# Spreading the pooling projections of a decoder block among the last heads' key and gate projections

## The chip, the cores and the metric

The kernel runs on one core of one Trainium2 chip (trn2). The metric is the device time of one execution in microseconds. A core has a matrix engine (PE, with its weight loads shown apart as PEld), a vector engine (DVE), a scalar engine (ACT), GpSimd (POOL) and a queue engine (SP) that here only issues transfers. Every engine works through its own instructions in a fixed order and waits, by semaphores, for what it needs from the others.

## The reference: one decoder block, 512 rows of width 1024

```python
h = rms_norm(x, g_mix);  u, q, k, v, gate_logits = split(h @ w_in)
y_pool = pool(u, w_pool) * pool_scale   # moving means over 2, 4, 8, 16 rows, minus u, then 128x128 weights, 4 groups
o      = diff_attention(rope(q), rope(k), v)   # 4 heads; softmax 1 - lam * softmax 2, causal
y_attn = rms_norm(o, g_subln) * (1 - lam_init)
x = x + (concat([y_pool, y_attn]) * sigmoid(gate_logits)) @ w_out
x = x + cross_attention(rms_norm(x), rms_norm(mem));  x = x + relu(rms_norm(x) @ w_up)**2 @ w_down
return rms_norm(x, g_final)
```

Everything is fp32. A product is made of three fp32r matmuls: both operands are split into a rounded high part and a low rest (`split`, lines 110 to 112: ACT writes the high part, DVE or POOL subtracts it for the low part), and `mm3` (lines 104 to 107) adds high x high, high x low and low x high.

## The kernel before

The part in question is the first quarter of the program. After the projection of v, twenty weight tiles follow, each a projection of all 512 rows to 128 columns: 24 matmuls of 128x512 into one of two `acc` banks. Their order is the string `PLAN`, read at line 302 and run by the loop at line 561: `k0` to `k3` and `q0` to `q3` are the heads' keys and queries, `u0` to `u3` the four pooling groups, `g0` to `g7` the gates (0 to 3 belong to the pooling groups, 4 to 7 to the heads). I number the tiles 0 to 19 by their place in `PLAN`.

What a tile is followed by:

- a key or query (`qk_proj`, lines 412 to 432): four ACT copies and one DVE product drain the bank, POOL makes two operations of the rotary embedding (lines 419, 420), ACT and DVE write the split pair `s`. For a key two transfers on SP (lines 430, 431) write a swapped copy `z`. All these live in six buffers with the tag `s`.
- a gate (`gate_proj`, lines 494 to 507): DVE line 498, ACT lines 500 to 502, DVE line 503, ACT line 504. `merge` (lines 509 to 514) multiplies it into its group's or head's result and splits the product: on POOL for groups 0 to 3, on DVE for the heads.
- a pooling group (`u_proj`, lines 524 to 545): DVE line 532 drains the bank, POOL adds shifted copies (line 537: 1, 2, 3 and 4 adds for groups 0 to 3), DVE line 540 and two narrow operations (lines 542, 543) finish the means, ACT and POOL split them. `u0` first calls `pool_weights` (lines 517 to 522): a transfer and a split of the pooling weights into an `s` buffer. 23 steps later `pool_mix` (lines 547 to 557) runs three matmuls into a `tr` bank, and ACT line 554 drains it.

The attention is laid between the tiles by a step counter. `tile_mm` counts one step for every three matmuls, so a tile has 8 steps; `after` (line 271) queues a function for a later step. With `START, SPACE, SOFTMAX, ATTEND, FINISH, POOLING = 20, 6, 15, 3, 6, 23` (line 32) the scores of head h and row block i stand at step 36 + 6(4h + i), their transposes (`flip`, line 456) 15 steps later, `attend` (line 469) 3 steps after a head's last flip, and `finish` (line 481) 6 steps after that. Scores write into three `sc` banks in turn, which DVE line 445 drains; a flip's transposes go to one of two `tr` banks, which ACT and DVE split into `at` (lines 465, 111, 112), and `attend` multiplies `at` with v. I write (h,i) for head h and row block i.

The order on PE is the order in which the program is written. The orders on the other engines and queues are set when the program is built. Weights come through three raw buffers and three split buffers (`load`, `prep`, `weights`, lines 155 to 213): at tile i the load of tile i+3 and the split of tile i+2 are asked for. The projection of the mixed result (`projection`, lines 580 to 595, called at line 662) follows the twentieth tile; its first three tiles take the parts 4, 5, 6, 0, 1 first and 2, 7, 3 last.

## Time and profile before

| | before |
|---|---|
| device time, three runs | 724.32, 724.35, 726.61 us; median 724.35 |
| the profiled execution: its own time, its span | 725.17 us, 723.4 us |
| DVE, ACT, POOL busy in the span | 513.1, 391.6, 72.9 us |
| DMA | 91.09 MB, mean 126 GB/s |
| line 105, 106, 107 `acc` matmuls of 128x512 on `whi`, `wlo` | 400 each, 395, 389, 390 ns |
| line 111 on ACT (`whi`, 94 of them), line 112 on DVE (`wlo`, 94) | mean 1035 ns, 1229 ns |

The span runs from the first to the last instruction of the profiled execution; 1.77 us of its own time lie around it. Matmuls overlap: one of 128x512 is shown with some 0.39 us, but the next one starts 0.23 us later, so on PE I read the distance between starts, not the durations. In a row of a timeline the first number is the start, the second the duration, and the bracket at the end gives the idle time before the instruction and who ended it. On DVE and ACT, too, the next instruction may start a little before the last one's shown end.

### The profile page before, as it was taken

What the parts mean: (1) busy time and instruction counts of PE and PEld (TensorE: products, weight loads), DVE (VectorE), ACT (ScalarE), POOL (GpSimd) and SP (SyncE); (2) the same over time, 40 slices, a digit from 0 to 9 for tenths busy, and PEclk for the clock granted to TensorE, in tenths of its full rate; (3) what the DMA queues carried; (4) which work ended last, traced back from release to release, by engine and by line L of the source; (5) the groups of instructions that cost most, each with busy time, mean ns of one, the idle gap of its engine ahead of it and who ended that gap; (6) DMA issues with size and microseconds to landing.
All of it is one profiled execution on the core that took longest, in us unless ns stands there. A gap on an engine that the chain in (4) does not pass through costs nothing.

```text
span 723.4 us, 10277 instructions
## 1 busy us (share of the span) xinstructions
PE 705.2 (97%) x3960; PEld 612.8 (85%) x3960; DVE 513.1 (71%) x798; ACT 391.6 (54%) x642; POOL 72.9 (10%) x66
## 2 busy tenths in 40 slices
PE   9999999999999999999999999999999999999993
PEld 6887888788889888888879978999889988899882
DVE  6698999975888545562899954598447963589426
ACT  7498998676766433452775641355214641355422
POOL 0044112534000000000000000000000000000003
PEclk9999999999999999999999999999999999999997
DMA  8443223143525552114835741548226651305003
GB/s 314 151 117 116 88 74 116 59 151 112 175 88 178 179 166 88 59 58 144 238 86 141 236 147 30 167 108 279 88 42 163 216 166 55 101 17 178 27 1 116
DMA packets 28256, 91.09 MB, mean 126 GB/s; under 512 B 3088, under 2 KB 5136, under 8 KB 28208
## 3 DMA queue, kind: packets, MB, share of 16 engines
q1 hardware_dynamic: 25856, 81.92, 33.7%
q0 software_dynamic: 2352, 8.52, 7.0%
q8 instruction: 31, 0.51, 0.3%
q14 instruction: 17, 0.14, 0.1%
HBM read 86.24 MB, written 2.10 MB: 122 GB/s over the span
## 4 chain that ended last, share of the span: by engine, by line
PE 78%; DVE 11%; ACT 4%; DMA 3%; issue 2%; POOL 0%; SPq 0%; DVEq 0%; ACTq 0%
PE acc L105 16%; PE acc L107 16%; PE acc L106 16%; PE sc L105 9%; PE sc L107 8%; PE sc L106 8%; DMA mraw<-wst 2%; DVE wlo L112 2%; DVE mix L112 1%; PE sc L386 1%; ACT tmp L447 1%; DVE mix L849 1%; PE sc L388 1%; PE sc L390 1%; DMA wraw<-wm 1%
## 5 line engine op out<-in xcount | busy, mean ns | idle before, releaser
L105 PE MATMUL acc<-xg,whi 128*128 128x512 f32 x400 | 158.2, 395 | 0.0
L107 PE MATMUL acc<-xg,wlo 128*128 128x512 f32 x400 | 156.1, 390 | 0.0
L106 PE MATMUL acc<-xg,whi 128*128 128x512 f32 x400 | 155.8, 389 | 0.0
L111 ACT CAST whi<-wraw 128x1024 fp32r<-128x1024 f32 (+1 forms) x94 | 97.1, 1035 | 106.5 <-PE acc L106 39.0
L112 DVE TENSOR_TENSOR wlo<-wraw,whi 128x1024 fp32r<-128x1024 f32 (+1 forms) x94 | 115.3, 1229 | 26.8 <-ACT whi L111 26.4
L107 PEld LDWEIGHTS acc<-xg,wlo 128*128 128x128 f32 x400 | 75.1, 188 | 16.1
L105 PEld LDWEIGHTS acc<-xg,whi 128*128 128x128 f32 x400 | 75.2, 188 | 14.7
L106 PEld LDWEIGHTS acc<-xg,whi 128*128 128x128 f32 x400 | 75.2, 188 | 14.5
L572 DVE TENSOR_TENSOR vr<-acc,vr 128x512 f32<-128x512 f32 x41 | 28.3, 691 | 82.3 <-PE acc L107 82.3
L164 POOL DMA_DIRECT2D mraw<-wst x16 | 13.8, 861 | 429.6 <-DMA mraw<-wst 292.2
L105 PE MATMUL sc<-mix,whi 128*128 128x256 f32 (+1 forms) x184 | 54.2, 294 | 0.0
L107 PE MATMUL sc<-mix,wlo 128*128 128x256 f32 (+1 forms) x184 | 54.0, 293 | 0.0
L106 PE MATMUL sc<-mix,whi 128*128 128x256 f32 (+1 forms) x184 | 53.9, 293 | 0.0
L111 ACT CAST whi<-mraw 128x1024 fp32r<-128x1024 f32 x24 | 25.0, 1051 | 43.3 <-PE acc L106 30.7
L885 DVE TENSOR_TENSOR tmp<-sc,tmp 128x512 f32<-128x512 f32 x56 | 37.7, 689 | 6.4 <-PE sc L107 6.3
L106 PE MATMUL acc<-xg,mhl 128*128 128x512 f32 x104 | 40.6, 390 | 0.2 <-DVE xg L112 0.2
L105 PE MATMUL acc<-xg,mhl 128*128 128x512 f32 x104 | 40.6, 391 | 0.0
L107 PE MATMUL acc<-xg,mhl 128*128 128x512 f32 x104 | 40.5, 390 | 0.0
L111 ACT CAST mhl<-wraw 128x1024 fp32r<-128x1024 f32 x19 | 20.0, 1053 | 33.9 <-PE acc L106 18.0
L107 PEld LDWEIGHTS sc<-mix,wlo 128*128 128x128 f32 x184 | 34.6, 188 | 1.1
L105 PEld LDWEIGHTS sc<-mix,whi 128*128 128x128 f32 x184 | 34.5, 188 | 1.0
L106 PEld LDWEIGHTS sc<-mix,whi 128*128 128x128 f32 x184 | 34.4, 187 | 1.1
(269 smaller groups left out, 1696.4 us busy)
## 6 DMA issues: line engine op xcount, KB each, us to landing
wraw<-wm SPq DMA_DIRECT2D x76, 512.0 KB, 3.6
mraw<-wst SPq DMA_DIRECT2D x24, 512.0 KB, 3.6
wraw<-wckv SPq DMA_DIRECT2D x16, 512.0 KB, 3.8
mraw<-wst POOLq DMA_DIRECT2D x16, 512.0 KB, 5.8
wraw<-wst SPq DMA_DIRECT2D x16, 512.0 KB, 3.7
s<-s SPq DMA_DIRECT2D x8, 256.0 KB, 3.7
vr<-xT SPq DMA_DIRECT2D x8, 256.0 KB, 4.8
outT<-mix SPq DMA_DIRECT2D x8, 256.0 KB, 2.2
```

Of the source, the lines that this page charges most:

```text
L105: nc.tensor.matmul(o, lh, rh, start=start, stop=False)
L106: nc.tensor.matmul(o, lh, rl, start=False, stop=False)
L107: nc.tensor.matmul(o, ll, rh, start=False, stop=stop)
L111: S.copy(hi, src)
L112: eng.tensor_tensor(lo, src, f(hi), op=ALU.subtract)
L164: nc.gpsimd.dma_start(r, part(n, then), accum_op=ALU.add)
L386: nc.tensor.matmul(o[i], xg[k][0][:, tb], wh[:, c], start=k == 0, stop=False)
L388: nc.tensor.matmul(o[i], xg[k][1][:, tb], wh[:, c], start=False, stop=False)
L390: nc.tensor.matmul(o[i], xg[k][0][:, tb], wl[:, c], start=False, stop=k == KC - 1)
L447: S.activation(e[:, :n], e[:, :n], AF.Exp, bias=mn, scale=-1.0, accum_out=sm[:, c:c + 1])
L572: V.tensor_tensor(t, o, t, op=ALU.add)
L885: V.tensor_tensor(u[new], o, u[old], op=ALU.add)
```

## The change

One string is written in another order.

```diff
-PLAN = "k0 q0 q1 k1 q2 q3 g4 k2 g5 g6 k3 g7 u0 u1 u2 u3 g0 g1 g2 g3"
+PLAN = "k0 q0 q1 k1 q2 q3 g4 k2 g5 u0 k3 g6 u1 g7 u2 g0 u3 g1 g2 g3"
```

Tiles 0 to 8, tile 10 (`k3`), tile 14 (`u2`) and the last three keep their places. `u0` moves from tile 12 to 9, `u1` from 13 to 12, `u3` from 15 to 16; `g6` from 9 to 11, `g7` from 11 to 13, `g0` from 16 to 15. The step numbers of the attention stay as they are. Nothing is added or left out: each engine has as many instructions as before. The matmuls of `pool_mix` for group 0 move with `u0` from step 127 to step 103, that is from behind the scores (3,3) to ahead of the scores (3,0). On the other engines the instructions behind the moved tiles change places. Three such places:

The first is on DVE, around the drains of the score banks of (3,0), `sc_322` and `sc_325` before. `tr_329` is the flip of (2,2), `acc_316` the tile `u1`, `wlo_340` the low part of the weights of tile 15, `tmp_307` the result of head 1.

```order
L112 TENSOR_TENSOR at_296_1216<-tr_329_1337,at_295_1215 128x3x128
L532 TENSOR_TENSOR padu_330_1346<-acc_316_1285,rstd_61_315 128x512
L445 ISA tmp_323_1313,small_324_1314<-sc_322_1310,cst_2_68 128x128
L445 ISA small_324_1314 128x1
L511 TENSOR_TENSOR tmp_307_1252<-tmp_307_1252,gate_219_925 128x512
L112 TENSOR_TENSOR wlo_340_1367<-wraw_317_1286,whi_339_1366 128x1024
L445 ISA tmp_326_1320,small_327_1321<-sc_325_1317,cst_2_68 128x128
```

The same place now: the banks of (3,0) are `sc_329` and `sc_332`, `tr_336` is the flip of (2,2), `acc_323` the tile `g7`, `tmp_311` head 1's result, `wlo_342` the low part of the weights of tile 16.

```order
L112 TENSOR_TENSOR at_300_1222<-tr_336_1352,at_299_1221 128x3x128
L498 TENSOR_TENSOR gate_337_1361<-acc_323_1300,rstd_61_315 128x512
L225 SCALAR_TENSOR_TENSOR tmp_311_1258<-tmp_312_1259,tmp_311_1258 128x512
L531 MEMSET padu_403_1615 128x16
L112 TENSOR_TENSOR wlo_342_1373<-wraw_324_1301,whi_341_1372 128x1024
L445 ISA tmp_330_1328,small_331_1329<-sc_329_1325,cst_2_68 128x128
L445 ISA small_331_1329 128x1
L511 TENSOR_TENSOR tmp_311_1258<-tmp_311_1258,gate_219_925 128x512
L445 ISA tmp_333_1335,small_334_1336<-sc_332_1332,cst_2_68 128x128
```

The first drain of (3,0) stood ahead of the weights' low part and stands behind it now; the two drains stand closer together.

The second is on DVE, a little later, around the low part of the flip of (2,3), the last that `attend` of head 2 needs (`tr_349` before, `tr_351` now). `acc_337` before and `acc_339` now are the tile `u2`. Before:

```order
L112 TENSOR_TENSOR at_296_1216<-tr_349_1404,at_295_1215 128x4x128
L531 MEMSET padu_393_1556 128x16
L452 SCALAR_TENSOR_TENSOR tmp_323_1313<-tmp_323_1313,small_321_1309,tmp_326_1320 128x128
L445 ISA tmp_343_1380,small_344_1381<-sc_342_1377,cst_2_68 128x256
L445 ISA small_344_1381 128x1
L532 TENSOR_TENSOR padu_364_1458<-acc_337_1363,rstd_61_315 128x512
```

Now:

```order
L503 SCALAR_TENSOR_TENSOR gate_337_1361<-gate_337_1361,tmp_338_1363 128x512
L452 SCALAR_TENSOR_TENSOR tmp_330_1328<-tmp_330_1328,small_328_1324,tmp_333_1335 128x128
L532 TENSOR_TENSOR padu_366_1464<-acc_339_1369,rstd_61_315 128x512
L112 TENSOR_TENSOR at_300_1222<-tr_351_1410,at_299_1221 128x4x128
L445 ISA tmp_355_1430,small_356_1431<-sc_354_1427,cst_2_68 128x384
```

The flip's low part stood ahead of the drain of tile `u2` and stands behind it now.

The third is on POOL, from the first add of group 3 (`padu_393` before, `padu_403` now) to the merges of groups 0 and 1. Before:

```order
L537 TENSOR_TENSOR pad_394_1559<-padu_393_1556 128x512
L537 TENSOR_TENSOR pad_395_1562<-pad_394_1559 128x512
L537 TENSOR_TENSOR pad_396_1565<-pad_395_1562 128x512
L537 TENSOR_TENSOR pad_397_1568<-pad_396_1565 128x512
L112 TENSOR_TENSOR tmp_400_1576<-tmp_398_1571,tmp_399_1575 128x512
L511 TENSOR_TENSOR s_392_1551<-s_392_1551,gate_409_1626 128x512
L112 TENSOR_TENSOR mix_411_1635<-s_392_1551,mix_411_1635 128x512
```

Now:

```order
L537 TENSOR_TENSOR pad_404_1618<-padu_403_1615 128x512
L511 TENSOR_TENSOR s_315_1278<-s_315_1278,gate_394_1561 128x512
L537 TENSOR_TENSOR pad_405_1621<-pad_404_1618 128x512
L112 TENSOR_TENSOR mix_396_1570<-s_315_1278,mix_396_1570 128x512
L537 TENSOR_TENSOR pad_406_1624<-pad_405_1621 128x512
L537 TENSOR_TENSOR pad_407_1627<-pad_406_1624 128x512
L112 TENSOR_TENSOR tmp_410_1635<-tmp_408_1630,tmp_409_1634 128x512
```

Group 0's merge, two instructions, stood behind group 3's adds and stands between them now. On DVE, group 3's lines 540, 542 and 543 now stand directly ahead of the low part of head 3's squares, which `finish` of head 3 needs; before, five instructions stood between.

## The prediction

> **What bounds the kernel now.** I read the page's busy shares first, then PE's waits between 80 and 200 us, where the moved tiles lie, then PE's order of time around each wait.

> ```profile
> PE 705.2 (97%) x3960; PEld 612.8 (85%) x3960; DVE 513.1 (71%) x798; ACT 391.6 (54%) x642; POOL 72.9 (10%) x66
> PEclk9999999999999999999999999999999999999997
> ```

> PE is busy 97% of the span at a granted clock of 0.9 or more in all slices but the last. The change gives PE the same matmuls in another order, so all that it can win or lose is waiting.

> ```profile
> PE sc L442 <- DVE small L445: 1.0, 2, 0.7
> PE av L106 <- DVE at L112: 0.7, 2, 0.4
> ```

> Four waits for DVE: two of scores for a free bank, two of `attend` for a flip's low part. Idle time hides the cost of restarting the pipeline, so I read the starts:

> ```profile
> 107.56 0.40 PE L105 MATMUL av<-at,vr 128*128 128x512 f32 x1
> 108.28 0.50 PE L106 MATMUL av<-at,vr 128*128 128x512 f32 x1 [0.33 <-DVE at L112]
> ...
> 124.95 0.28 PE L442 MATMUL sc<-s,s 128*128 128x256 f32 x1
> 125.07 0.28 PE L443 MATMUL sc<-s,s 128*128 128x256 f32 x1
> 125.55 0.38 PE L442 MATMUL sc<-s,s 128*128 128x256 f32 x1 [0.20 <-DVE small L445]
> ...
> 130.49 0.33 PE L442 MATMUL sc<-s,s 128*128 128x384 f32 x1
> 130.66 0.34 PE L443 MATMUL sc<-s,s 128*128 128x384 f32 x1
> 131.75 0.44 PE L442 MATMUL sc<-s,s 128*128 128x384 f32 x1 [0.75 <-DVE small L445]
> ...
> 148.33 0.39 PE L107 MATMUL acc<-xg,wlo 128*128 128x512 f32 x1
> 148.56 0.40 PE L105 MATMUL acc<-xg,whi 128*128 128x512 f32 x1
> ```

> A matmul of 512 columns takes 0.23 us from start to start (148.33 to 148.56), of 256 columns 0.12, of 384 columns 0.17. Against these steps the waits cost 0.72 - 0.23 = **0.49** (attend of head 1), 0.48 - 0.12 = **0.36** (second scores of (3,1)) and 1.09 - 0.17 = **0.92** (second scores of (3,2)): 1.77 us together. The fourth wait, at 85 us in attend of head 0, lies ahead of the first moved tile and stays.

> ```profile
> 80.00:100.00 20.00, 19.59 (x97) 16.07 (x97) 17.43 (x43) 19.73 (x45) 2.59 (x2) 1.00 0.32 93
> 100.00:120.00 20.00, 19.67 (x96) 16.22 (x95) 18.77 (x42) 19.48 (x40) 3.81 (x3) 1.00 0.33 103
> 120.00:140.00 20.00, 19.05 (x95) 15.65 (x94) 18.74 (x56) 12.04 (x29) 10.64 (x8) 1.00 0.25 83
> ```

> The columns are the stretch and its length, then busy time of PE, PEld, DVE, ACT, POOL, then the clock. From 80 to 120 us ACT has 39.2 of 40 us, from 100 to 140 DVE has 37.5 of 40. These two set PE's waits; the clock is 1.00 through all of them.

> **The change, part by part.**

> *Fewer ACT operations ahead of attend of head 1.* `g6`, with four ACT operations, leaves tile 9; `u0` brings one (and the split of the pooling weights another) in its place. ACT, 99% busy there, gets to the last flip of head 1 sooner, though DVE then still has the low part of head 0's product ahead of it. That gives between 0 and the 0.49; I take 0.4 of it.

> *The drains of (3,0).* The second scores of (3,1) write into the bank of the first scores of (3,0), so they wait for the first drain.

> ```profile
> 116.80 0.68 DVE L112 TENSOR_TENSOR s<-wraw,s 128x512 fp32r<-128x512 f32 x1
> ...
> 118.61 1.22 DVE L112 TENSOR_TENSOR wlo<-wraw,whi 128x1024 fp32r<-128x1024 f32 x1
> 119.74 0.42 DVE L112 TENSOR_TENSOR at<-tr,at 128x256 fp32r<-128x256 f32 x1
> 120.76 0.68 DVE L540 SCALAR_TENSOR_TENSOR tmp<-pad,padu 128x496 f32<-128x496 f32 x1 [0.53 <-POOL pad L537]
> ...
> 125.21 0.28 DVE L445 CUSTOM_DVE_ANT_0 tmp<-sc,cst 128x128 f32<-128x128 f32 x1
> ...
> 126.02 2.07 DVE L112 TENSOR_TENSOR wlo<-wraw,whi 128x1024 fp32r<-128x1024 f32 x1
> ...
> L537 POOL TENSOR_TENSOR pad<-pad x6: 1039/1336/1903, 127.1 to 147.4; 128x512 f32<-128x512 f32 x6
> L537 POOL TENSOR_TENSOR pad<-padu x4: 1052/1740/1961, 118.8 to 143.1; 128x512 f32<-128x512 f32 x4
> ```

> Before, that drain starts at 125.21. Counted from the scores (2,3), three things differ ahead of it. The split of the pooling weights is gone, 0.60 us to the next start. The low part of a 1024-wide weight tile is ahead of it now: 1.13 us (118.61 to 119.74). And line 540, for which DVE waited for POOL here already (0.53 us), now waits for group 1's two adds instead of group 0's one: one add more, 1.04 to 1.90 us, median 1.34. Drain lines 532 and 498 take each other's place at the same price. So the drain comes 1.13 - 0.60 + 1.34 = 1.87 us later against the work ahead. PE wants the bank later too, by the three matmuls of `pool_mix` that now stand ahead: 0.68 us. The wait becomes 0.36 + 1.87 - 0.68 = **1.55** us instead of 0.36. With the fast and the slow add it is 1.25 or 2.11; if the low part is also stretched as at 126.02 (2.07 instead of 1.22, beside POOL's adds), 2.96. If ACT's relief brought the whole queue 1.55 us forward, it would be 0.

> *The second scores of (3,2)* need the first drain of (3,1). Both drains of (3,0) now stand close together behind the low part, and (3,1)'s come next, while PE has 18 matmuls (4.1 us) to go to its need: the 0.92 goes.

> *Attend of head 2* waits for the flip's low part, which now stands behind the drain of `u2`, the tile that PE ends just ahead of the scores (3,2) and the attend.

> ```profile
> 163.52 0.39 PE L107 MATMUL acc<-xg,wlo 128*128 128x512 f32 x1
> 164.02 0.69 DVE L498 TENSOR_TENSOR gate<-acc,rstd 128x512 f32<-128x512 f32 x1 [0.67 <-PE acc L107]
> ...
> 107.55 0.68 DVE L112 TENSOR_TENSOR at<-tr,at 128x512 fp32r<-128x512 f32 x1
> ```

> An idle DVE starts such a drain 0.50 us after the tile's last matmul starts. With 0.60 for the drain and 0.73 from the low part's start to PE's (107.55 to 108.28), line 106 starts 1.83 us after that last matmul. Unhindered, PE is there after 0.23 + 4 x 0.17 + 0.23 = 1.14. New wait: **0.69** us, 0 if DVE finds the bank early for another delay of PE, and not much more, since DVE has caught up here.

> *Group 3's adds and finish of head 3.* On POOL the merge of group 0 now cuts into these adds; on DVE line 540 waits for the last add; ACT's copy of the means and DVE's low part of head 3's squares stand behind it, and PE's line 235 needs the latter.

> ```profile
> 161.45 0.39 PE L235 MATMUL tr<-tmp,ones 128*128 128x512 f32 x1
> ...
> 143.14 1.96 POOL L537 TENSOR_TENSOR pad<-padu 128x512 f32<-128x512 f32 x1 [1.18 <-DVE padu L532]
> 145.18 3.87 POOL L537 TENSOR_TENSOR pad<-pad 128x512 f32<-128x512 f32 x3
> ...
> 155.60 1.30 POOL L112 TENSOR_TENSOR tmp<-tmp,tmp 128x512 fp32r<-128x512 f32 x1 [6.55 <-ACT tmp L111]
> 160.83 1.29 POOL L511 TENSOR_TENSOR s<-s,gate 128x512 f32<-128x512 f32 x1 [3.94 <-ACT gate L504]
> ```

> `u3` is tile 16 now; tile 16's last matmul starts at 148.33, line 235 at 161.45: 13.1 us of cover. The chain: 0.50 and 0.60 to the drain's end, the adds 5.9 us (143.14 to 149.05), the merge's two instructions 1.3 each, then 0.8 on DVE, three ACT operations of about 0.5, and 0.6 on DVE again: 13.5 us by these rows, and so a wait of **0.4**. With all adds at 1.04 the chain is 11.8 and covered; with all at 1.96 it is 15.4, a wait of 2.3.

> *Transfers and buffers at no cost.* All six `s` buffers are full when `k3`'s swapped copy is made, since the pooling weights came first; it takes `k2`'s buffer and waits on SP for the scores (2,3), with the next weight loads queued behind it. The copy for `k2` already lives like this:

> ```profile
> 92.07 0.47 SPq L430 DMA_DIRECT2D s<-s  x1
> 92.59 0.59 SPq L431 DMA_DIRECT2D s<-s  x1
> ...
> 96.91 0.27 PE L443 MATMUL sc<-s,s 128*128 128x128 f32 x1
> ...
> DMA to landing us min/median/max: 3.0/3.9/4.5
> ```

> The second half, issued at 92.59, is needed at 96.91, 4.3 us later, and came in time; `k3`'s has 0.68 us more for `pool_mix`, 5.0 us against the slowest landing of 4.5. Without that cover it would cost what is missing, a few tenths. The weights' loads behind it are two tiles (11 us) ahead of PE. The next projection needs the merges:

> ```profile
> 167.23 1.29 POOL L112 TENSOR_TENSOR mix<-s,mix 128x512 fp32r<-128x512 f32 x1 [1.83 <-ACT mix L111]
> ...
> 169.19 0.40 PE L105 MATMUL sc<-mix,whi 128*128 128x512 f32 x1
> ```

> Group 1's ends at 168.5; PE starts at 169.19 and wants group 1 twelve matmuls (2.7 us) later, so 3.4 us cover it, and its wait behind group 3's split on POOL costs nothing up to there. `g2` and `g3`, which rule the last merges, keep their places.

> **Sum.** Gone: 0.4 + 0.36 + 0.92 = 1.68. New: 1.55 + 0.69 + 0.4 = 2.64. Net **+0.96 us**: the profiled execution's own 725.17 (span 723.4) would become 726.1. It lies 0.8 above the median of the three runs, so for the median I say 724.35 + 0.96 = **725.3 us**. From no change a measurement can tell here only what exceeds 0.3%, 2.2 us.

> **Rivals.**

> *Relief.* ACT and DVE gain so much by `g6`'s move that the new waits are covered. Then only the three old ones go: 724.35 - 1.77 = 722.6. For it speaks ACT's 99%; against it that DVE's place behind POOL's second add and behind `u2`'s drain doesn't depend on ACT. It cannot reach 0.3% without a gain that no row shows.

> *POOL and DVE in each other's way: slower.* POOL is nearly idle before 118 us (2.6 and 3.8 of 20 us); now groups 0 and 1 add there while DVE is 94% busy, and group 3 adds beside the merge. If these overlaps stretch the adds to 1.9 and the low part to 2.07, the waits are 2.96 + 0.69 + 2.3 = 5.95, less 1.68: +4.3, or 728.6. It is slower by more than 2.2 us from new waits of 3.9 us on; half of the stretch does it. For it speaks that adds of one form take 1.04 to 1.96; against it that half of those between two pads are at 1.34 or less. [...]

> *No effect.* The places differ, but DVE's and ACT's sums don't, and PE's waits only change names: 724.35 +- 0.5.

> **How the numbers follow.** Forecast (+0.2 to +2.0) 0.50; no effect 0.14; relief (-0.5 to -1.8) 0.14; POOL against DVE (+2.0 to +4.3) 0.22. Faster by over 0.3% needs more than relief gives: 0.03. Slower by over 0.3%: 0.20. Within: 0.77. For the range I leave out the last microsecond of the slow case and the full relief: 722.9 to 727.5.

> **What would show it.** In the changed kernel's waits of PE: no wait at the second scores of (3,2); one of 1.2 to 2.1 us at the second scores of (3,1) behind DVE's drain, whose row follows a `wlo`; 0.7 at `attend` of head 2, released by `at` line 112; a small one at line 235; line 540 of group 1 waiting for POOL. PE's waits behind 170 us as before. I am wrong if PE waits for `z` (a transfer) at the scores (3,0), for weights, or at the next projection for a merge.

## The result, and the profile after

| | before | after |
|---|---|---|
| device time, median of 4 runs (lowest to highest) | 724.34 us (724.01 to 726.61) | 733.39 us (730.53 to 734.93) |
| the profiled execution: its own time, its span | 725.17, 723.4 us | 734.56, 732.8 us |
| DVE, ACT, POOL busy in the span | 513.1, 391.6, 72.9 us | 517.6, 391.4, 73.7 us |

The changed kernel is slower: the ratio is 1.0114, with a 95% interval of 1.0099 to 1.0130. PE has the same matmuls, so the 9 us are waiting or slower matmuls. These are PE's waits between 80 and 200 us in the changed kernel (engine and line, who was waited for, us in total, times, longest):

```profile
PE sc L442 <- DVE small L445: 3.1, 1, 3.1
PE av L106 <- DVE pad L536: 1.5, 1, 1.5
PE av L106 <- DVE at L112: 0.9, 2, 0.5
PE tr L463 <- DVE tmp L452: 0.8, 1, 0.8
PE tr L234 <- ACT tmp L111: 0.5, 1, 0.5
PE tr L235 <- DVE tmp L112: 0.3, 1, 0.3
```

Before, the waits were 1.7 us in four places; now they are 7.1 us in seven. As in the prediction I read what a wait costs between starts, less the usual step. (A correction to the list of DVE's order above: the low part `wlo_340` belongs to tile 16, as `wlo_342` does, not to tile 15. So it is the same split that changed places with the drain.)

**The second scores of (3,1).** PE's order of time:

```profile
127.90 0.28 PE L443 MATMUL sc<-s,s 128*128 128x256 f32 x1
131.24 0.38 PE L442 MATMUL sc<-s,s 128*128 128x256 f32 x1 [3.06 <-DVE small L445]
...
132.27 0.40 PE L105 MATMUL acc<-xg,whi 128*128 128x512 f32 x1
132.50 0.53 PE L106 MATMUL acc<-xg,whi 128*128 128x512 f32 x1
132.83 0.63 PE L107 MATMUL acc<-xg,wlo 128*128 128x512 f32 x1
133.25 0.63 PE L105 MATMUL acc<-xg,whi 128*128 128x512 f32 x1
```

3.34 us lie between the two starts instead of 0.12: 3.22 lost. Then something that none of the waits shows: from 132.5 us on the matmuls start 0.42 us apart instead of 0.23. The table by stretches (length, then PE, PEld, DVE, ACT, POOL busy, granted clock, DMA share, GB/s) shows why:

```profile
128.00:132.00 4.00, 0.94 (x6) 0.72 (x5) 4.00 (x10) 0.78 (x3) 1.26 (x1) 1.00 0.05 4
132.00:136.00 4.00, 4.00 (x14) 3.18 (x14) 2.65 (x11) 3.92 (x12) 0.00 (x0) 0.58 0.40 131
```

The granted clock is 0.58 in the four microseconds behind the wait: 4 x 0.42 = 1.7 us lost with PE busy all the time. DVE and POOL on the way to that drain:

```profile
121.98 2.11 DVE L112 TENSOR_TENSOR wlo<-wraw,whi 128x1024 fp32r<-128x1024 f32 x1 [1.15 <-ACT whi L111]
...
125.01 0.66 DVE L540 SCALAR_TENSOR_TENSOR tmp<-pad,padu 128x496 f32<-128x496 f32 x1
...
128.11 1.73 DVE L225 SCALAR_TENSOR_TENSOR tmp<-tmp,tmp 128x512 f32<-128x512 f32 x1
129.78 1.20 DVE L112 TENSOR_TENSOR wlo<-wraw,whi 128x1024 fp32r<-128x1024 f32 x1
...
130.90 0.28 DVE L445 CUSTOM_DVE_ANT_0 tmp<-sc,cst 128x128 f32<-128x128 f32 x1
...
120.85 1.04 POOL L537 TENSOR_TENSOR pad<-padu 128x512 f32<-128x512 f32 x1 [11.43 <-DVE small L450]
121.97 1.04 POOL L537 TENSOR_TENSOR pad<-pad 128x512 f32<-128x512 f32 x1
128.03 1.26 POOL L112 TENSOR_TENSOR tmp<-tmp,tmp 128x512 fp32r<-128x512 f32 x1 [5.02 <-ACT tmp L111]
```

The kernel before had, undisturbed:

```profile
123.53 0.69 DVE L225 SCALAR_TENSOR_TENSOR tmp<-tmp,tmp 128x512 f32<-128x512 f32 x1
```

The reader is to see four things: DVE waits 1.15 us for ACT, in whose rows line 554, the drain of group 0's `pool_mix` that the change brought here, stands shortly ahead with 0.67 us; the low part of tile 15 takes 2.11 us, begun beside an add of POOL, where the prediction's row has 1.22; line 225 takes 1.73 us, begun beside POOL's low part, where it took 0.69 before; and the low part of tile 16 stands ahead of the drain. Line 540, begun at 125.01, does not wait for POOL: the two adds took 1.04 us each and were done at 123.01. Counted from the scores (2,3), the drain comes 3.57 us later than before (14.47 against 10.90) and PE's need for it 0.71 us later: 0.36 + 3.57 - 0.71 = 3.22.

**The flip (2,0)**, of which the prediction does not speak:

```profile
113.00 0.69 DVE L426 TENSOR_TENSOR s<-tmp,s 64x512 fp32r<-64x512 f32 x1
113.72 0.75 DVE L452 SCALAR_TENSOR_TENSOR tmp<-tmp,small,tmp 128x128 f32<-128x128 f32 x2
...
114.22 0.30 PE L463 MATMUL tr<-cst,tmp 128*128 128x128 f32 x1 [0.79 <-DVE tmp L452]
```

The last step of the softmax of (2,0), line 452, stands behind both low parts of `k3`'s split (lines 424, 426) on DVE; before, it stood ahead of them:

```profile
105.31 0.54 DVE L452 SCALAR_TENSOR_TENSOR tmp<-tmp,small,tmp 128x128 f32<-128x128 f32 x1
...
111.07 0.69 DVE L424 TENSOR_TENSOR s<-tmp,s 64x512 fp32r<-64x512 f32 x1
```

In the changed kernel PE's last start ahead of this was 113.04, so 0.95 us are lost.

**Attend and finish of head 3**, DVE, POOL and PE:

```profile
157.53 1.53 DVE L511 TENSOR_TENSOR tmp<-tmp,gate 128x512 f32<-128x512 f32 x1
158.98 2.32 DVE L112 TENSOR_TENSOR wlo<-wraw,whi 128x1024 fp32r<-128x1024 f32 x1
161.22 1.52 DVE L112 TENSOR_TENSOR mix<-tmp,mix 128x512 fp32r<-128x512 f32 x1
162.67 0.68 DVE L112 TENSOR_TENSOR at<-tr,at 128x512 fp32r<-128x512 f32 x1
...
157.16 1.35 POOL L537 TENSOR_TENSOR pad<-padu 128x512 f32<-128x512 f32 x1 [9.39 <-DVE padu L532]
158.47 1.74 POOL L511 TENSOR_TENSOR s<-s,gate 128x512 f32<-128x512 f32 x1
160.18 2.02 POOL L537 TENSOR_TENSOR pad<-pad 128x512 f32<-128x512 f32 x1
162.16 1.72 POOL L112 TENSOR_TENSOR mix<-s,mix 128x512 fp32r<-128x512 f32 x1
163.84 3.27 POOL L537 TENSOR_TENSOR pad<-pad 128x512 f32<-128x512 f32 x2
...
163.40 0.50 PE L106 MATMUL av<-at,vr 128*128 128x512 f32 x1 [1.51 <-DVE pad L536]
...
169.97 0.51 PE L234 MATMUL tr<-tmp,ones 128*128 128x512 f32 x1 [0.52 <-ACT tmp L111]
170.72 0.50 PE L235 MATMUL tr<-tmp,ones 128*128 128x512 f32 x1 [0.25 <-DVE tmp L112]
```

From 157 to 163 us DVE and POOL take turns: three DVE instructions need 5.4 us, which at 0.68, 1.22 and 0.68 would need 2.6. Attend of head 3 loses 1.68 us for that (the memset named as releaser ends beside the low part of the flip, begun at 162.67, which is what `attend` needs), and finish of head 3 loses 1.20.

### The profile page after: what moved, and what is told of

Its sections match the earlier page's. It is cut to its first block, busy times and chain, and to the rows that moved or that the text cites. A ratio compares the mean times of both kernels' runs of the same rounds, so it can differ in the third digit from the quotient of the medians.

```text
span 732.8 us, 10277 instructions
## 1 busy us (share of the span) xinstructions
PE 708.7 (97%) x3960; PEld 614.4 (84%) x3960; DVE 517.6 (71%) x798; ACT 391.4 (53%) x642; POOL 73.7 (10%) x66
## 4 chain that ended last, share of the span: by engine, by line
PE 85%; DVE 7%; ACT 4%; issue 2%; DMA 1%; POOL 0%; DVEq 0%; SPq 0%; ACTq 0%; POOLq 0%
PE acc L105 17%; PE acc L106 17%; PE acc L107 17%; PE sc L105 9%; PE sc L107 9%; PE sc L106 9%; DVE wlo L112 1%; PE sc L386 1%; PE sc L388 1%; ACT whi L111 1%; DVE tmp L885 1%; PE sc L390 1%; DVE mix L849 1%; DMA wraw<-wm 1%; ACT tmp L447 1%
## 5 line engine op out<-in xcount | busy, mean ns | idle before, releaser
L105 PE MATMUL acc<-xg,whi 128*128 128x512 f32 x400 | 158.7, 397 | 0.0
L107 PE MATMUL acc<-xg,wlo 128*128 128x512 f32 x400 | 156.6, 391 | 0.0
L106 PE MATMUL acc<-xg,whi 128*128 128x512 f32 x400 | 156.3, 391 | 0.0
L111 ACT CAST whi<-wraw 128x1024 fp32r<-128x1024 f32 (+1 forms) x94 | 97.1, 1034 | 108.2 <-PE acc L106 40.3
L112 DVE TENSOR_TENSOR wlo<-wraw,whi 128x1024 fp32r<-128x1024 f32 (+1 forms) x94 | 117.8, 1255 | 29.5 <-ACT whi L111 28.9
L107 PEld LDWEIGHTS acc<-xg,wlo 128*128 128x128 f32 x400 | 75.4, 188 | 16.3
L106 PEld LDWEIGHTS acc<-xg,whi 128*128 128x128 f32 x400 | 75.5, 189 | 14.7
L105 PEld LDWEIGHTS acc<-xg,whi 128*128 128x128 f32 x400 | 75.5, 189 | 14.6
L105 PE MATMUL sc<-mix,whi 128*128 128x256 f32 (+1 forms) x184 | 54.2, 294 | 0.0
L107 PE MATMUL sc<-mix,wlo 128*128 128x256 f32 (+1 forms) x184 | 54.0, 293 | 0.0
L106 PE MATMUL sc<-mix,whi 128*128 128x256 f32 (+1 forms) x184 | 53.9, 293 | 0.0
L111 ACT CAST whi<-mraw 128x1024 fp32r<-128x1024 f32 x24 | 25.0, 1051 | 44.4 <-PE acc L106 32.2
L885 DVE TENSOR_TENSOR tmp<-sc,tmp 128x512 f32<-128x512 f32 x56 | 37.5, 684 | 6.4 <-PE sc L107 6.3
L106 PE MATMUL acc<-xg,mhl 128*128 128x512 f32 x104 | 40.6, 390 | 0.2 <-DVE xg L112 0.2
L105 PE MATMUL acc<-xg,mhl 128*128 128x512 f32 x104 | 40.6, 391 | 0.0
L107 PE MATMUL acc<-xg,mhl 128*128 128x512 f32 x104 | 40.5, 389 | 0.0
L111 ACT CAST mhl<-wraw 128x1024 fp32r<-128x1024 f32 x19 | 20.0, 1052 | 35.6 <-PE acc L106 18.0
L107 PEld LDWEIGHTS sc<-mix,wlo 128*128 128x128 f32 x184 | 34.6, 188 | 1.1
L105 PEld LDWEIGHTS sc<-mix,whi 128*128 128x128 f32 x184 | 34.5, 188 | 1.0
L106 PEld LDWEIGHTS sc<-mix,whi 128*128 128x128 f32 x184 | 34.4, 187 | 1.1
```

The costliest lines, as they stand in the source:

```text
L105: nc.tensor.matmul(o, lh, rh, start=start, stop=False)
L106: nc.tensor.matmul(o, lh, rl, start=False, stop=False)
L107: nc.tensor.matmul(o, ll, rh, start=False, stop=stop)
L111: S.copy(hi, src)
L112: eng.tensor_tensor(lo, src, f(hi), op=ALU.subtract)
L885: V.tensor_tensor(u[new], o, u[old], op=ALU.add)
```

## The experiments

**u3 and g0 back in their old places:**

```diff
-PLAN = "... u1 g7 u2 g0 u3 g1 g2 g3"
+PLAN = "... u1 g7 u2 u3 g0 g1 g2 g3"
```

> The changed kernel with u3 and g0 in their old places (tiles 15 and 16); u0, u1, g6 and g7 stay moved. Theory (each new wait belongs to its place: DVE's order there, stretched by POOL's adds beside it): the waits of PE at attend of head 3 (1.51 us idle) and at lines 234 and 235 of head 3 (0.77 together) go, those at the flip (2,0), the second scores of (3,1) and attend of head 2 stay, with the slow matmuls behind (3,1). That takes 1.68 + 1.20 = 2.9 us from 733.4: 730.5, a ratio of 1.0085 to the kernel before. Rival (the loss hangs on the one long wait at (3,1) and on a start that differs between executions; the waits behind it only follow from it): 732.5 to 734, ratio 1.011 to 1.013. Rival (all hangs on u3 and g0): 724 to 726.

Measured: 729.98 us, ratio 1.0071 (1.0049 to 1.0093). Attend of head 3 and lines 234 and 235 don't wait; (2,0), (3,1) with 3.06 us idle and the slow matmuls, and attend of head 2 are as they were. So the waits belong to their places, and the later ones don't follow from the long one.

**Only u3 and g0 exchanged, in the kernel before:**

```diff
-PLAN = "... u0 u1 u2 u3 g0 g1 g2 g3"
+PLAN = "... u0 u1 u2 g0 u3 g1 g2 g3"
```

> The kernel before with only u3 and g0 exchanged (u3 tile 16, g0 tile 15). Theory of places: the waits at attend of head 3 and at lines 234 and 235 of head 3 come alone, 1.5 to 3 us together, the three old waits stay, the clock stays at 1.00: 726 to 727.3, ratio 1.002 to 1.004. Rival (these waits only follow from the long wait ahead): 724.3, ratio 1.000.

Measured: 726.52 us, ratio 1.0024 (1.0011 to 1.0036). The three old waits stay, attend of head 3 loses 0.76 us and line 235 0.82, 1.6 together. The exchange costs what the theory says by itself.

**Group 3 without its adds on POOL**, in the changed kernel:

```diff
-            nc.gpsimd.tensor_tensor(nxt[:, PAD:], cur[:, PAD:], cur[:, PAD - step:PAD + T - step], op=ALU.add)
-            cur, step = nxt, 2 * step
+            if g != 3:
+                nc.gpsimd.tensor_tensor(nxt[:, PAD:], cur[:, PAD:], cur[:, PAD - step:PAD + T - step], op=ALU.add)
+                cur = nxt
+            step = 2 * step
```

> The changed kernel without group 3's four adds on POOL (line 537 left out for that group, so that its mean is wrong); everything else stands as it was. Theory (POOL's adds beside DVE's two-input instructions stretch both): of DVE's line 511, the weights' low part and the low part of head 2's product, which take 1.53, 2.32 and 1.52 us ahead of the last flip of head 3, at least two come back to 0.7, 1.2 and 0.7; PE's wait at attend of head 3 goes from 1.51 us to under 0.3, those at lines 234 and 235 to under 0.3 too; 733.4 - 2.5 = about 730.9, ratio 1.009. Rival (the order alone makes the wait): the three durations and the 1.5 us at attend stay, only the waits at lines 234 and 235 go: 732.2, ratio 1.011.

Measured: 729.96 us, ratio 1.0067 (1.0045 to 1.0089). The same stretch on DVE and POOL (lines 542 and 544 are 540 and 542 of the other kernels):

```profile
154.67 0.69 DVE L511 TENSOR_TENSOR tmp<-tmp,gate 128x512 f32<-128x512 f32 x1
155.27 1.22 DVE L112 TENSOR_TENSOR wlo<-wraw,whi 128x1024 fp32r<-128x1024 f32 x1
156.41 0.67 DVE L542 SCALAR_TENSOR_TENSOR tmp<-padu 128x496 f32<-128x496 f32 x1
156.99 1.29 DVE L544 TENSOR_TENSOR tmp<-padu,cst 128x16 f32<-128x16 f32 x1
...
155.49 2.75 POOL L511 TENSOR_TENSOR s<-s,gate 128x512 f32<-128x512 f32 x1 [10.24 <-ACT gate L504]
```

Lines 511 and the low part are back at 0.69 and 1.22, the wait at attend of head 3 falls to 0.16, and those at 234 and 235 go. What is left of POOL's work shows the kind of the overlap: POOL's line 511, begun at 155.49 in the middle of a DVE instruction that ended at 156.49, took 2.75 us instead of 1.29; the 1.46 more are, by the starts, the rest of that instruction, 0.92, and the next one, 0.58. DVE's 16 columns wide instruction, caught behind it, took 1.29 instead of 0.17 and ended at 158.28, just behind POOL's 158.24. By these rows, one waited for the whole of the other; it is an overlap of the kind that the prediction's second rival prices.

**One order on DVE set, at (3,1)**, in the changed kernel (`issue_after` queues the low part behind a named instruction of the same engine and adds no wait):

```diff
+            st["d", h, i, c] = V.tensor_tensor_reduce(...)
...
-            split(hi, lo, r, G if i in WPOOL else V)
+            with tc.issue_after(st["d", 3, 0, 1].ins) if i == 20 else nullcontext(): split(hi, lo, r, V)
```

> The changed kernel with one order set on DVE: the low part of the weights of tile 16 stands behind both drains of the scores (3,0) and not ahead of them; the low part of the last flip of head 2 then comes ahead of the drain of u2 as well. Theory (DVE's order sets the wait, and a wait this long also costs the clock): PE's wait at the second scores of (3,1) falls by the 1.12 us of that low part, from 3.06 to 1.9 us; the wait at attend of head 2 (0.45) goes; and the matmuls behind (3,1), which went at 0.42 us from start to start for 4 us, go at 0.23: 1.1 + 0.6 + 1.65 = 3.3 us, 730.1, ratio 1.008. Rival (the slow matmuls have a cause of their own, not this wait): they stay, and the time falls by 1.7 only: 731.7, ratio 1.010. Rival (the drain waits for POOL or ACT anyway): 3.06 us stays.

Measured: 729.80 us, ratio 1.0077 (1.0049 to 1.0106), and as expected an idle time of 1.93 us, no wait at attend of head 2, fast matmuls behind. The low part of tile 16 in the drain's way accounts for 1.13 us.

**The wait filled with eight matmuls**, in the changed kernel:

```diff
-            o = ps("sc", 3)
+            j = ps("av", 1) if (h, i, c) == (3, 1, 1) else None; [nc.tensor.matmul(j, ones, xg[0][0], start=True, stop=True) for _ in range(8 if j else 0)]; o = ps("sc", 3)
```

> The changed kernel with eight more matmuls of 128x512 between the first and the second scores of (3,1), where PE waits 3.06 us: they multiply tiles that lie ready into the free bank of the head products and their result is not used. Every other engine has the same order as in the changed kernel. Theory (the long idle time itself slows the matmuls behind it): the eight take 1.8 us out of the wait, the idle time falls to about 1.2 us, the matmuls behind it go at 0.23 us from start to start instead of 0.42, and the clock in that stretch is 1.00: with more work the kernel gets 1.6 us faster, 731.8, ratio 1.009. Rival (the slow matmuls come from something else in that stretch, such as the transfers or DVE's drains): they stay at 0.42, 733.4, ratio 1.0114. Rival (the wait is not idle time that can be filled): 735.2.

Measured: 731.91 us, ratio 1.0100 (1.0077 to 1.0123), idle time 1.26 us, matmuls 0.23 us apart behind it. It came as expected, but see the runs on the beat below: one profile with fast matmuls would not have been enough.

**Group 1's low part on POOL cut to 16 columns**, in the changed kernel:

```diff
-        sp = split_sq(z, T, ZLO_E)
+        sp = split_sq(z, T, ZLO_E) if g != 1 else (tmp(F32R), tmp(F32R)); g == 1 and (S.copy(sp[0], z), ZLO_E.tensor_tensor(sp[1][:, :PAD], z[:, :PAD], f(sp[0][:, :PAD]), op=ALU.subtract))
...
-        mm3(y, st["wp"][:, 0, c], st["wp"][:, 1, c], sp[0], sp[1], True, True)
+        mm3(y, st["wp"][:, 0, c], st["wp"][:, 1, c], sp[0], sp[1] if g != 1 else sp[0], True, True)
```

> The changed kernel, in which POOL writes only 16 of the 512 columns of the low part of group 1's means, and the matmul that would read them reads the high part (so group 1's means are not exact). DVE's order up to the scores (3,1) is that of the changed kernel. Theory (DVE's line 225 of head 1 takes 1.73 us because POOL's low part of 1.26 us starts beside it): line 225 takes 0.7 us, PE's wait at the second scores of (3,1) falls from 3.06 to 2.0 us, and as that is short enough the slow matmuls go too: 1.05 + 1.65 = 2.7 us, 730.7, ratio 1.0077. Rival (line 225 is slow for a reason of its own, such as its operands): 1.73 and 3.06 us stay, 733.4, ratio 1.0114.

Measured: 730.28 us, ratio 1.0074 (1.0055 to 1.0094).

```profile
125.83 0.68 DVE L225 SCALAR_TENSOR_TENSOR tmp<-tmp,tmp 128x512 f32<-128x512 f32 x1
126.46 1.20 DVE L112 TENSOR_TENSOR wlo<-wraw,whi 128x1024 fp32r<-128x1024 f32 x1
...
127.92 0.39 PE L442 MATMUL sc<-s,s 128*128 128x256 f32 x1 [2.02 <-DVE small L445]
```

Line 225 takes 0.68 us and the idle time falls from 3.06 to 2.02: POOL's low part made 1.04 us of the wait. In one point the expectation missed: the matmuls behind the 2.02 us went slow here (clock 0.57 from 128 to 132 us), though 1.93 us had not done that.

**Lines 451 and 452 of (2,0) ahead of k3's split**, in the changed kernel, by the same means (`"a"` and `"b"` hold the two instructions of each softmax):

```diff
-        S.copy(s[top, 0, :], a[top, :])
-        V.tensor_tensor(s[bot, 0, :], a[top, :], f(s[top, 0, :]), op=ALU.subtract)
+        with tc.issue_after(st["a", 2, 0].ins) if (which, h) == ("k", 3) else nullcontext(): S.copy(s[top, 0, :], a[top, :])
+        with tc.issue_after(st["b", 2, 0].ins) if (which, h) == ("k", 3) else nullcontext(): V.tensor_tensor(s[bot, 0, :], a[top, :], f(s[top, 0, :]), op=ALU.subtract)
```

and so for the other half.

> The changed kernel with one order set on ACT and one on DVE: lines 451 and 452 of (2,0) stand ahead of the split of k3 (lines 423 to 426), as they do in the kernel before. With that the orders behind move too: the first drain of (3,0) stands ahead of the low part of the weights of tile 16, the flip's low part of (2,3) ahead of the drain of u2. Theory (the orders of DVE and ACT make the waits): the wait at the flip (2,0), 0.95 us, goes; the wait at (3,1) falls to 2 us or less, as by setting the drain alone; the slow matmuls and the wait at attend of head 2 go: 0.95 + 1.1 + 1.65 + 0.6 = 4.3 us, 729.1, ratio 1.0055. Rival (the waits at (3,1) and attend of head 2 come with the tiles' places, whatever the order): 0.95 goes, 732.4, ratio 1.010.

Measured: 726.90 us in ten runs (726.51 to 731.12), ratio 1.0033 (1.0016 to 1.0050), better than expected. The profile is of the slowest of the ten, 731.12 us. In it the waits at (2,0), attend of head 2 and attend of head 3 are gone and that at (3,1) is 1.02 us. Ordering these two lines by hand at 113 us takes 6.5 of the 9 us away in the median. The profile shows one way in which it does so: the orders that are set behind them, when the program is built, come out otherwise, and the first drain of (3,0) stands ahead of the low part of tile 16 again. The delay of head 3 comes in this profile at lines 234 and 235, most of it at 234:

```profile
151.47 3.69 POOL L537 TENSOR_TENSOR pad<-padu 128x512 f32<-128x512 f32 x1 [8.72 <-DVE padu L532]
...
164.74 0.50 PE L234 MATMUL tr<-tmp,ones 128*128 128x512 f32 x1 [2.66 <-ACT tmp L111]
```

Here DVE ran its instructions undisturbed (0.68 us for 512 columns, 1.22 for the weights' low part at 152.44), and POOL's first add paid: 3.69 us. The nine faster executions have no profile, so whether they lost as much there is not shown.

**Nine orders set**, in the changed kernel. `keep` notes instructions by name, and each pair of `PINS` queues the second behind the first:

```diff
+PINS = [(('half',2,0),('shi','k',3)), (('half',2,0),('shi2','k',3)), (('p',2,0),('slo','k',3)), (('p',2,0),('slo2','k',3)), (('drain',3,0,0),('gate',7)), (('drain',3,0,0),('y',1)), (('drain',3,0,1),('wlo',16)), (('at',2,3),('u',2)), (('at',3,3),('mlo',2))]
+keep = lambda *k: (kept.update({k[:-1]: k[-1].ins}), [tc.add_manual_dep(kept[b], kept[a].name, order, reason="order") for a, b in PINS if k[:-1] in (a, b) and a in kept and b in kept])
```

> The changed kernel with nine orders set on ACT and DVE: (2,0)'s lines 451 and 452 ahead of k3's split; the first drain of (3,0) ahead of line 498 of g7 and line 225 of head 1, the second ahead of the low part of the weights of tile 16; the low part of the flip (2,3) ahead of the drain of u2; the low part of the flip (3,3) ahead of the low part of head 2's product. Theory (the loss lies in these orders, not in the tiles' places): the waits at the flip (2,0), at (3,1), and at attend of heads 2 and 3 are each under 0.5 us, the slow matmuls are gone, only lines 234 and 235 of head 3 wait some 1.2 us: 733.4 - 0.9 - 2.9 - 1.65 - 0.6 - 1.3 = 726, ratio 1.002. Rival (with the tiles in these places DVE and ACT have more to do in the stretch than they can, so that the waits come back elsewhere): 729 to 731, ratio 1.006 to 1.009.

Measured: 726.62 us, ratio 1.0018 (1.0005 to 1.0031). The tiles lie where the change put them, and from 100 to 150 us no wait is left; attend of head 3 loses 0.78, where under 0.5 was expected, and lines 234 and 235 lose 1.7. So there is room enough in the places; the orders on ACT and DVE carried the loss ahead of 150 us, and group 3's chain on POOL what is behind.

**Three and eight orders set, in the kernel before**, to see whether its own waits can be had:

```diff
+PINS = [(('at',1,3),('mlo',0)), (('drain',3,0,0),('y',1)), (('drain',3,1,0),('wlo',16))]
```

> The kernel before, its tiles in their old places, with three orders set on DVE: the low part of head 0's product behind the low part of the flip (1,3), line 225 of head 1 behind the first drain of (3,0), and the low part of the weights of tile 16 behind the first drain of (3,1). Theory (each of the three old waits of PE, 0.49, 0.36 and 0.92 us, is made by the instruction that stood ahead on DVE): all three go, no new one of over 0.3 us comes: 724.4 - 1.8 = 722.6, ratio 0.9976. Rival (DVE is so full there that what is put behind is late next, and PE waits for that): 724 to 725, ratio 1.000.

Measured: 723.88 us, ratio 0.9987 (0.9976 to 0.9998). Attend of head 1 and (3,1) don't wait; (3,2) still loses 1.12 us, because the drain of (3,1) is still late.

```diff
+PINS = [(('athi',0,3),('g504',4)), (('athi',0,3),('half',1,0)), (('at',0,3),('drain',1,1,0)), (('at',1,3),('mlo',0)), (('drain',3,0,0),('y',1)), (('drain',3,1,0),('wlo',16)), (('drain',3,1,0),('at',2,3)), (('drain',3,1,0),('u',2))]
```

> The kernel before with eight orders set on ACT and DVE: the orders of the run with three, but the first drain of (3,1) also ahead of the low part of the flip (2,3) and of line 532 of u2; and the two parts of the flip (0,3) ahead of line 504 of g4 and line 451 of (1,0) on ACT and of the first drain of (1,1) on DVE. Theory (each wait is made by what stood ahead): beside the waits at attend of head 1 and at (3,1), those at (3,2) (1.1 us in the run with three) and at attend of head 0 (0.67) go: 724.7 - 0.5 - 0.4 - 0.9 - 0.67 = 722.3, ratio 0.9966. Rival (something put behind is late next): as with three orders, 723.9, ratio 0.9987.

Measured: 723.56 us, ratio 0.9988 (0.9977 to 0.9998). (3,2) is down to 0.16, but attend of head 2, whose low part was put behind, loses 1.06 now, and head 0's wait moved to the scores behind it (0.44). Both are faster than both kernels, by 0.12 to 0.13% of the kernel before, no more: on a DVE that is 94% busy (37.5 of the 40 us from 100 to 140 in the kernel before; 37.0 and 38.8 with three and eight orders), what was put behind was late next.

**Four and five matmuls in the wait, twice each, and the changed kernel again.** The edit is that of the eight, with 4 or 5.

> The changed kernel with four more matmuls, not eight, in the wait at (3,1). The idle time becomes 2.15 us. Theory (the length of the idle time decides, with a limit between 1.93, where the matmuls behind it stayed fast, and 2.02, where they went slow): slow matmuls at 0.42 us behind it, as without fillers. Rival (it depends on where the wait falls against a beat of the clock's own, so lengths near 2 go either way): fast here, or slow in one profile and not in the other.

> The changed kernel with five more matmuls in the wait at (3,1). The idle time becomes 1.92 us. Theory (a limit of length between 1.93 and 2.02): no slow matmuls. Rival (a beat): either.

> The changed kernel with four added matmuls again: idle time 2.15 us. With a beat that differs between executions it may be slow here, where it was fast in the first profile; without one it is fast again.

> The changed kernel with five added matmuls in the wait at (3,1) again, for a second profile: idle time 1.92 to 1.95 us. Rival to a limit of length (a beat): the same kernel can go the other way, fast behind the wait where it was slow in the first profile. If it is slow again, the length and the place in the program decide, not a beat that differs between executions.

> The changed kernel again, for a second profile. Theory (the 1.73 us that the first profile lost in the program's first 9 us are a matter of the execution, and the waits and the slow matmuls of the change): the start is that of the kernel before within 0.5 us, and the start-to-start excess between 104 and 175 us is again 7 to 8 us. Rival (the change moved the start too): the start is slow again, 1.7 us.

Measured, in this order and in two runs each: medians of 732.52, 734.91, 734.62, 732.51 and 732.75 us. PE's rows at the wait with four matmuls, from the first profile:

```profile
128.59 0.39 PE L442 MATMUL sc<-s,s 128*128 128x256 f32 x1 [2.16 <-DVE small L445]
...
128.94 0.39 PE L105 MATMUL acc<-xg,whi 128*128 128x512 f32 x1
129.17 0.39 PE L106 MATMUL acc<-xg,whi 128*128 128x512 f32 x1
```

and from the second profile of the same kernel:

```profile
129.30 0.58 PE L442 MATMUL sc<-s,s 128*128 128x256 f32 x1 [2.16 <-DVE small L445]
...
129.89 0.63 PE L105 MATMUL acc<-xg,whi 128*128 128x512 f32 x1
130.32 0.63 PE L106 MATMUL acc<-xg,whi 128*128 128x512 f32 x1
```

The same idle time, and 0.23 us from start to start the first time, 0.43 the second. The granted clock of the four microseconds behind the wait, from the table by stretches of each profile, and, in brackets, PE's idle time in the fullest window of the clock's beat on which the wait falls, of which more below:

| | idle time | first profile | second profile |
|---|---|---|---|
| four matmuls in the wait | 2.16 us | 1.00 (1.75 us) | 0.57 (1.99 us) |
| five matmuls in the wait | 1.95 us | 0.60 (1.95 us) | 1.00 (1.83 us) |
| the changed kernel | 3.06 us | 0.58 (2.05 us) | 1.00 (1.57 us) |

The clock of the last entry, and a later stretch of the same profile that is used below, in the table by stretches of the second profile of the changed kernel:

```profile
130.00:134.00 4.00, 4.00 (x21) 3.30 (x20) 2.65 (x12) 4.00 (x12) 0.00 (x0) 1.00 0.39 135
383.00:387.00 4.00, 4.00 (x23) 4.00 (x24) 4.00 (x7) 2.46 (x4) 0.00 (x0) 0.61 0.34 108
```

So the length alone does not decide. What differs between the executions is how the wait falls on a beat, and the traces' records of the granted clock show the beat. In each of the 17 profiles, every stretch at 1.00 between its first record and the drop at the program's end lasts a whole number of windows of 3.413 us (36 windows, 122.88 us, up to the drop in the first profile of the changed kernel, 111 in the second, and 207 windows, 706.56 us, in the kernel before), and each drop ahead of the last 20 us lasts one such window, at 0.50. If a profile is cut into these windows, PE's idle time in one is the window's length less PE's busy time. The 3.06 us of the changed kernel fell on two windows with 1.01 and 2.05 us in the first profile and with 1.57 and 1.49 us in the second. Over all of some 3,550 windows, leaving out the last 20 us of each program, every one of the thirteen drops follows a window with 1.66 to 2.72 us of idle time, and only two other windows have more than 1.66 us: 1.75 and 1.83 us, the two fast entries with four and five matmuls. So in these profiles it is idle time within one window that goes with a drop, from 1.66 us, about half of the window, on. This is read from the profiles; no run sets where the windows lie.

The start was the execution's too: the first profile of the changed kernel reached its 50th matmul 1.73 us later than the kernel before, the second 0.12 us earlier. In the first, matmuls start 0.43 us apart until 9.15 us, in the second only until 3.73 us. So the start came as expected; the 7 to 8 us of excess behind 104 us did not, since the slow matmuls stayed away: it is 6.1 us.

The two profiles with four matmuls differ behind 150 us as well. In the first, DVE and POOL take turns, attend of head 3 loses 1.68 us and lines 234 and 235 lose 1.2; in the second, POOL's first add takes 3.69 us, attend of head 3 loses nothing and lines 234 and 235 lose 3.45. So which of DVE and POOL pays differs between executions of one kernel, and group 3's chain ends late either way.

## Why the prediction was wrong

The forecast was +0.96 us, 725.3 within 722.9 to 727.5; the medians differ by 9.05. The terms, from the first profile of the changed kernel, with nothing of start or clock in them:

| place | predicted | measured |
|---|---|---|
| attend of head 1; second scores of (3,2) | -0.4; -0.92 | -0.49; -0.92 |
| second scores of (3,1) | 1.55 for 0.36 | 3.22 for 0.36 |
| attend of head 2 | +0.69 | +0.61 |
| finish of head 3 | +0.4 (0 to 2.3) | +1.20 |
| flip (2,0) | not seen | +0.95 |
| attend of head 3 | not seen | +1.68 |
| sum | +0.96 | +5.9 |
| slow matmuls behind (3,1) | not seen | +1.7 in three of four profiles with that wait, 0 in one |

As a check on the sum: in the second profile, without slow matmuls, PE loses 6.1 us against the kernel before between its 450th and 750th matmul; in the first, 7.6.

- *"The 0.92 goes"* and the 0.69 at attend of head 2: right in mechanism and nearly in size; DVE starts the drain of `u2` 0.42 us behind the tile's last matmul start, and the flip's low part directly behind it. The relief at attend of head 1 was right in size, but little of it came at the flip itself: counted from the transposes, ACT's high part of the flip is only 0.13 us earlier, its high part of head 0's product 0.55 us earlier, and with that DVE's low part of that product, which stands ahead of the flip's.
- *"The wait becomes 0.36 + 1.87 - 0.68 = 1.55"* is the step that failed. Its mechanism, the low part ahead of the drain, was right and worth its 1.13 us (the run with the drain first). But the 1.34 us for "one add more" did not come at all, as line 540 didn't wait for POOL, and the 0.53 us for which it had waited before went too. In its place came 1.04 us on line 225 (shown by the run with 16 columns), 0.9 us on a low part of tile 15, and 1.15 us in which DVE waited for ACT; the last two are read from the rows and weren't tried by themselves. I had named POOL as somebody to wait for, where it was somebody to share with.
- *Finish of head 3, 0.4 with all adds at their rows' time*: the chain was the right one, but took longer. POOL's four adds and the merge's two instructions ran from 157.16 to 167.11, 9.95 us against 5.9 + 2.6 in the working, and the drain of `u3` came late behind DVE's queue, 1.73 us behind the tile's last matmul start instead of 0.50. The working also has a slip in its sum: the terms that it lists add up to 12.5 us, not 13.5, so by its own rows the chain was covered with 0.6 us to spare, and the forecast would have been +0.56. That the 0.4 lies nearer to the measured 1.20 is no merit of the working.
- *Attend of head 3* was a place the working never looked at: it followed what stands behind POOL's adds, not which DVE instructions run beside them. Without the adds the first two of the three take 0.69 and 1.22 us instead of 1.53 and 2.32, and the wait is 0.16. As the profiles with four matmuls show, this loss and that at finish of head 3 are split otherwise in other executions.
- *The flip (2,0)* was missed because the orders on DVE were compared at three places, of which this was none. The run that sets this order shows more: the orders behind it, (3,1)'s among them, hang on it.
- *The rival "POOL and DVE in each other's way"* was the right one in kind, priced at +4.3 and given 0.22. Its own sum already had 2.96 at (3,1) and 2.3 at the finish; it lacked (2,0), attend of head 3 and the clock. That its 2.96 lies near the 3.22 is in part chance: it has the stretch in the adds, at 1.9, and in the low part ahead of the drain, at 2.07, and these took 1.04 and 1.20; line 225, the low part of tile 15 and ACT came in their place.
- *"The clock is 1.00 through all of them"* was true before, and taken for a constant. Here 1.66 us of idle time within one window of 3.413 us were enough to end that.

Of the list of what would show it: no wait at (3,2), the `wlo` ahead of the drain, 0.6 at attend of head 2, waits for no transfer, weight or merge, and nothing new in PE's waits behind 175 us came out as listed; the size at (3,1) and line 540 did not.

Not settled: the medians differ by 9.05 us, the first profile's terms and slow matmuls give 7.6. Starts of different length (1.85 us between the two profiles of the changed kernel), and further stretches of lower clock are larger than the rest of 1.4 us, but how often they come in the timed runs was not measured.

## What to carry to other kernels

Where one engine is as busy as DVE here (94% of a stretch) and orders are set by a scheduler, compare its order over the whole stretch, not only where the tiles move, since one early exchange can turn the later ones. An engine that is mostly idle, as POOL is here (73.7 of 732.8 us busy), can still cost: before moving its work beside a busy one, find rows in which the two overlap and price every overlap, whichever of them has to wait. A wait of PE that can put some 1.7 us of idle time into one window of 3.413 us should be priced at its length plus a chance of the clock's drop behind it: in these runs 13 of the 15 windows with 1.66 us or more of idle time had one behind them, at 1.7 us more each.
